# Layer 0 of a two-layer backbone: v and the output gate computed with tokens as the stationary operand, two heads at a time

## The chip, the core and the metric

The kernel runs on one core of a Trainium2 chip (trn2). The metric is the device time of one execution in microseconds (us). The kernel before took 1768.49 us, the median of three runs (1768.12 to 1774.79). The engines are named as the profile names them: PE (TensorE, matrix products; PEld is its weight load), DVE (VectorE), ACT (ScalarE), POOL (GpSimd) and SP (SyncE, which issues most of the DMAs).

## The reference, cut to what matters

512 latent tokens and 256 context tokens of width 2048 pass two layers; everything is float32. The change lies in layer 0 alone:

```
proj = xm @ w_in                       # xm: modulated tokens, 512 latent and 256 context
q, k, v, o, z_m, gates, u_p, z_p = split(proj)   # q, k, v, o, z_m: 4 heads x 256 columns each
q, k = silu(conv3(q)), silu(conv3(k))  # over three neighbouring tokens, channel by channel
h  = mlstm(q, k, v, gates)             # both directions; latent tokens also read the context's k, v
h  = h * sigmoid(o);  h = normalize(h) * g;  y_m = h * silu(z_m)
r  = multiscale_pool(u_p) - u_p        # 4 groups x 256 columns
y_p = (r @ pool_w) * pool_scale * silu(z_p)
x  = layer_norm(alpha * x + gate * (concat(y_m, y_p) @ w_out))
```

Layer 1 (a gated MLP with its own two large products) is not touched. Only the latent stream is returned, so of the context layer 0 needs k and v alone.

## The kernel before, in words

**Products on split operands.** A float32 product is made of three faster ones. `split` (L103 to L106) writes the rounded part of an operand as a `fp32r` tile (hi, on ACT, L105) and the rest as another (lo, on DVE, L106). A product is then hi·hi + hi·lo + lo·hi, three matmuls into one PSUM bank. A PSUM bank holds 128 x 512 float32; there are eight.

**Two forms.** `form_a` (L174 to L191) keeps a 128 x 128 block of weights as the stationary operand and moves tokens past it: 512 latent columns (`xh`, `xl`) and, where asked, 256 context columns (`cy`). Its result lies channels by tokens. `form_b` (L193 to L223) keeps 128 tokens as the stationary operand and moves 512 columns of weights: its result lies tokens by channels, one PSUM bank for each group of 128 tokens. Before the change `form_b` serves only the output products of both layers (L201 to L203).

**The weight stream.** The list `stream` fixes the order in which weights come from HBM, 512 KB a piece. `ahead` (L151 to L172) keeps three pieces in flight (tag `wraw`) and splits two halves of a piece ahead of the product that uses them (tag `whl`, four buffers).

**Layer 0.** While the tokens are being modulated (the first 228 us) some blocks of q, k and v are formed beside it, the list `nb1`. Then `kv_products` forms k and v of the context, and for heads 2 and 3 those of the latent tokens with them, and stores them in DRAM (`kcd`, `vcd`, `h2d`). v comes out channels by tokens and must lie tokens by channels, so `v_out` turns it by PE transposes, 128 x 128 each (L472), and splits the result. Then come the four heads. Each loads or forms q and k, forms u, o, z_m and z_p by `form_a`, and runs `attention`, `finish` and `pooling` beside these products. o is turned by PE transposes too (L724). `pooling` ends in four plain float32 products (L782) which the profile lists as two matmul records each.

**What sets the order.** `Flow` interleaves the tasks by a count of PE time: a task that yields 4.0 goes on when products worth 4 us have been emitted. A scheduler then fixes each engine's order with a simulation of its own, and gives tiles their buffers; on the chip every engine runs its list strictly in that order. `ada` is a task that streams the modulation weights of the next stages (`adat`, 512 KB for every 2.8 us of PE time at first) past a DVE multiply (L280).

**After layer 0** come its output product, layer 1's products and the final output product; their code is unchanged, but line numbers move.

## Time and profile before

| | |
|---|---|
| median of three runs | 1768.49 us |
| the profiled execution | 1771.65 us, of which span 1769.9 us |
| PE busy | 1725.7 us, 98% of the span |
| DVE busy | 1168.8 us, 66% |
| ACT busy | 686.7 us, 39% |
| chain that ended last | PE 78%, DMA 12%, DVE 7%, issue 2%, ACT 1% |
| HBM traffic | 340.93 MB read, 22.07 MB written, 205 GB/s over the span |

The profile comes from one execution, so sums made from it are set against its own 1771.65 us. Matmuls are pipelined: the duration of one record reaches into the next, so the cost of a matmul is the distance from its start to the next start. The profile's mean duration of a 128 x 512 matmul is some 390 ns, but such matmuls start every 227 ns. The span falls into the modulation stage (0 to 227.8 us), the context products of head 0 (227.8 to 256.4), the other products of `kv_products` (256.4 to 394.6), the four heads (394.6 to 898.5) and the rest.

### The profile page before, as it was taken

The page shows a single profiled execution, that of the slowest core. Times are in us where ns is not written, and L with a number is a line of the kernel's source. Part 1 is how long each engine was busy: PE and PEld are TensorE (multiplying, and loading weights), DVE is VectorE, ACT ScalarE, POOL GpSimd, SP SyncE. Part 2 cuts the span into 40 slices and gives each one's busy share as a digit, 9 for nine tenths or more (in the row PEclk, how much of TensorE's full clock was granted, in tenths as well). Part 3 has the DMA queues.
Part 4 walks back from the last instruction along what each step waited for, and adds up shares of the span by engine and source line. Part 5 has one row for each costly group of instructions (what it writes and reads, how often), then busy time and mean ns, then how long its engine had stood idle before and what let it go on. Part 6 is the DMA issues. An engine that isn't in the chain of part 4 may idle for free.

```text
span 1769.9 us, 23424 instructions
## 1 busy us (share of the span) xinstructions
PE 1725.7 (98%) x8608; PEld 1415.4 (80%) x8608; DVE 1168.8 (66%) x2074; ACT 686.7 (39%) x1209; POOL 93.9 (5%) x129
## 2 busy tenths in 40 slices
PE   8999999999999999999999999989999999999996
PEld 5677788888788888888888888878887888788884
DVE  3545598678774676875654476856776767665557
ACT  3222332124454445345342237734454354432220
POOL 0000000000000000000000000121100001000004
PEclk9999999999999999999999999999999999999998
DMA  9986289899742364663275457897757575765442
GB/s 368 358 307 236 90 310 328 295 328 363 240 149 81 118 218 148 207 216 110 84 259 152 146 187 279 225 227 198 213 158 213 147 234 128 214 158 172 134 132 106
DMA packets 133817, 364.54 MB, mean 206 GB/s; under 512 B 13262, under 2 KB 23462, under 8 KB 133190
## 3 DMA queue, kind: packets, MB, share of 16 engines
q1 hardware_dynamic: 122182, 323.20, 53.5%
q0 software_dynamic: 9216, 33.56, 10.7%
q10 hardware_dynamic: 2304, 6.29, 0.9%
q8 instruction: 67, 1.10, 0.2%
q14 instruction: 48, 0.39, 0.1%
HBM read 340.93 MB, written 22.07 MB: 205 GB/s over the span
## 4 chain that ended last, share of the span: by engine, by line
PE 78%; DMA 12%; DVE 7%; issue 2%; ACT 1%; POOL 0%; SPq 0%; POOLq 0%; DVEq 0%; ACTq 0%
DMA adw<-in_adat_dram 7%; PE ps L1211 7%; PE ps L1210 7%; PE ps L1212 7%; PE ps L190 7%; PE ps L185 7%; PE ps L186 7%; PE ps L201 6%; PE ps L203 6%; PE ps L202 6%; DMA qr<-in_wq_dram 2%; DVE adw L280 2%; PE ps L408 2%; PE ps L410 2%; PE ps L409 2%; PE ps L640 2%
## 5 line engine op out<-in xcount | busy, mean ns | idle before, releaser
L105 ACT CAST wh<-wr 128x512 fp32r<-128x512 f32 x352 | 216.4, 621 | 427.9 <-PE ps L203 164.5
L106 DVE TENSOR_TENSOR wh<-wr,wh 128x512 fp32r<-128x512 f32 x344 | 235.0, 687 | 205.0 <-ACT wh L105 199.6
L185 PE MATMUL ps<-xh,wh 128*128 128x512 f32 x704 | 278.6, 396 | 0.0
L190 PE MATMUL ps<-xh,wh 128*128 128x512 f32 x704 | 275.4, 391 | 0.3 <-DVE wh L106 0.3
L186 PE MATMUL ps<-xl,wh 128*128 128x512 f32 x704 | 275.7, 392 | 0.0
L203 PE MATMUL ps<-wh,yl 128*128 128x512 f32 x512 | 199.5, 390 | 0.0
L201 PE MATMUL ps<-wh,yh 128*128 128x512 f32 x512 | 193.6, 391 | 0.0
L202 PE MATMUL ps<-wh,yh 128*128 128x512 f32 x480 | 187.2, 390 | 0.0
L280 DVE SCALAR_TENSOR_TENSOR adw<-adw,crow 128x1024 f32<-128x1024 f32 x128 | 156.1, 1221 | 43.7 <-DMA adw<-in_adat_dram 43.3
L190 PEld LDWEIGHTS ps<-xh,wh 128*128 128x128 f32 x704 | 132.4, 188 | 29.2 <-DVE wh L106 0.7
L1211 PE MATMUL ps<-wh,ch 128*128 128x512 f32 x384 | 150.1, 393 | 0.8 <-DVE wh L106 0.7
L185 PEld LDWEIGHTS ps<-xh,wh 128*128 128x128 f32 x704 | 132.8, 189 | 22.1 <-issue 0.7
L186 PEld LDWEIGHTS ps<-xl,wh 128*128 128x128 f32 x704 | 132.9, 189 | 21.6 <-issue 0.7
L1212 PE MATMUL ps<-wh,ch 128*128 128x512 f32 x384 | 149.3, 392 | 0.0
L1210 PE MATMUL ps<-wh,ch 128*128 128x512 f32 x384 | 144.2, 397 | 3.6 <-ACT wh L105 3.6
L105 ACT CAST wh<-qr 128x1024 fp32r<-128x1024 f32 x96 | 100.9, 1057 | 117.4 <-DMA qr<-in_wq_dram 57.3
L106 DVE TENSOR_TENSOR wh<-qr,wh 128x1024 fp32r<-128x1024 f32 x96 | 116.6, 1220 | 33.1 <-ACT wh L105 13.4
L106 DVE TENSOR_TENSOR wh<-pair,wh 128x1024 fp32r<-128x1024 f32 x72 | 87.9, 1221 | 56.7 <-ACT wh L105 18.3
L105 ACT CAST wh<-pair 128x1024 fp32r<-128x1024 f32 x72 | 75.7, 1052 | 107.5 <-PE ps L1212 39.4
L1211 PE MATMUL ps<-wh,xn 128*128 128x512 f32 x288 | 113.9, 396 | 0.7 <-DVE wh L106 0.7
L1212 PE MATMUL ps<-wh,xn 128*128 128x512 f32 x288 | 113.3, 393 | 0.0
L1210 PE MATMUL ps<-wh,xn 128*128 128x512 f32 x288 | 108.0, 399 | 4.3 <-ACT wh L105 4.3
(298 smaller groups left out, 2915.4 us busy)
## 6 DMA issues: line engine op xcount, KB each, us to landing
adw<-in_adat_dram SPq DMA_DIRECT2D x128, 512.0 KB, 5.8
qr<-in_wq_dram SPq DMA_DIRECT2D x112, 512.0 KB, 4.9
wr<-in_wie_dram SPq DMA_DIRECT2D x96, 512.0 KB, 4.4
aw<-in_a_dram SPq DMA_DIRECT2D x64, 512.0 KB, 7.2
pair<-in_wq_dram POOLq DMA_DIRECT2D x56, 512.0 KB, 7.1
wr<-in_woe_dram SPq DMA_DIRECT2D x40, 512.0 KB, 4.6
wr<-in_woo_dram SPq DMA_DIRECT2D x32, 512.0 KB, 3.8
w<-in_wie_dram SPq DMA_DIRECT2D x28, 256.0 KB, 5.6
```

The source lines that it names most:

```text
L105: sc.copy(hi, src)
L106: return ve.tensor_tensor(lo, src, f32(hi), ALU.subtract)
L185: te.matmul(pt[:, :n], a, xh_, start=first, stop=False)
L186: te.matmul(pt[:, :n], a, xl_, start=False, stop=False)
L190: te.matmul(pt[:, :n], b, xh_, start=False, stop=last)
L201: te.matmul(pts[t], a, wh, start=n == 0, stop=False)
L202: te.matmul(pts[t], a, wl, start=False, stop=False)
L203: te.matmul(pts[t], b, wh, start=False, stop=n == KB - 1)
L280: ve.scalar_tensor_tensor(ts[n], ts[n], 0.5, crow[k], ALU.mult, ALU.mult, accum_out=part[:, f % 4, k:k + 1])
L1210: te.matmul(pts[t], a, wh[:, s], start=first, stop=False, **more)
L1211: te.matmul(pts[t], a, wl[:, s], start=False, stop=False, **more)
L1212: te.matmul(pts[t], b, wh[:, s], start=False, stop=end, **more)
```

## The change

- v of heads 0 and 1 is formed in one `form_b` over all six groups of 128 tokens (two of context, four latent), 512 columns at once, and v of heads 2 and 3 in a second one (`v_products`). The result is split straight from PSUM and stored in DRAM (`vd`), from which each head loads its part. `v_copy`, `v_out`, `vl_out` and the transposes of v are gone.
- o is formed by `form_b` over the four latent groups, for heads 0 and 1 while head 0 is worked on, for heads 2 and 3 in head 2. The tanh goes from PSUM straight into `og`; `o_out` and its transposes are gone.
- The pooling product is made of split operands: six `fp32r` matmuls in place of two float32 ones for each of its two banks. Three more splits for each head make the operands.
- `nb1` holds q and k of heads 1 and 2 in place of v of head 0 and k, v, q of head 1. `k_products` forms k of heads 0 and 3 only; q of head 3 alone is formed in its head.
- z_p of head 0 moves into head 1, z_p of head 2 into head 3; weights of v and o lie in DRAM as whole rows (`wv`, `wo`), the stream follows the new order.

```diff
+    Z_M, U_P, Z_P = 16, 24, 32
+    stream = a_raws(io["wie"], 8) + a_raws(io["wie"], 9) + b_raws(io["wv"], 0)
+    stream += a_raws(io["wie"], 14) + a_raws(io["wie"], 15) + b_raws(io["wv"], 1)
...
-        nb1 = [16, 17, 10, 11, 18, 19, 2, 3]
+        nb1 = [2, 3, 10, 11, 12, 13, 4, 5]
...
         def ctx_in(h):
             for j in range(2):
                 dma.dma_start(f32(kT[h][j][2]), kcd[h][:, j])
-                dma.dma_start(f32(vv[h][j][0]), vcd[h][:, j])
+                for J2 in range(3):
+                    dma.dma_start(f32(vv[h][j][J2]), vd[h, J2][:, j])
...
-            yield 1.0
-            pv = ps()
-            for j in range(4):
-                te.transpose(pv[:, j * P:(j + 1) * P], to[:, j * P:(j + 1) * P], ident)
-            ve.tensor_copy(ogt[h][:, :, fb * P:(fb + 1) * P], pv.rearrange("p (j f) -> p j f", f=P))
...
+            pws = at.tile([P, 3, 2, 256], F32R, tag="aT", name=nm("pws"))
+            split(pwt, pws[:, 0], pws[:, 1])
...
+                split(r_.rearrange("p r c -> p (r c)"), *rr[fb])
...
-                for k2 in range(2):
-                    te.matmul(pt, pwt[:, k2, fb * P:(fb + 1) * P], rr[k2].rearrange("p r c -> p (r c)"),
-                              start=k2 == 0, stop=k2 == 1)
+                for n, (k2, a, b) in enumerate((k2, a, b) for k2 in range(2) for a, b in ((0, 0), (0, 1), (1, 0))):
+                    te.matmul(pt, pws[:, a, k2, fb * P:(fb + 1) * P], rr[k2][b], start=n == 0, stop=n == 5)
...
+        def x_stat(kb, t):
+            if t < 2:
+                return cy[kb][:, 0, t * P:(t + 1) * P], cy[kb][:, 1, t * P:(t + 1) * P]
+            return xh[kb][:, (t - 2) * P:(t - 1) * P], xl[kb][:, (t - 2) * P:(t - 1) * P]
+
+        def v_products(c):
+            for pts in form_b(range(6), x_stat, range(KB)):
+                for t, pt in pts.items():
+                    vs = at.tile([P, 2, 512], F32R, tag=("og", "zs", "b0")[t % 3], name=nm("vs"))
+                    split(pt, vs[:, 0], vs[:, 1])
+                    for i in range(2):
+                        sc.dma_start(vd[2 * c + i, t // 2][:, :, t % 2, :], f32(vs[:, :, i * 256:(i + 1) * 256]))
...
+            if h in (0, 3):
+                v_products(h // 3)
...
-            for b in (4, 5, 0, 1, 2, 3) if early else (2, 3, 4, 5, 0, 1):
-                fb, out_ = b % 2, (q_out, k_out, vl_out)[b // 2]
+            for b in (0, 1, 2, 3) if early else (2, 3, 0, 1):
+                fb, out_ = b % 2, (q_out, k_out)[b // 2]
...
+                ogt[h // 2] = at.tile([P, 4, 512], F32, tag="og", name=nm("og"))
+                for pts in form_b(range(NT), lambda kb, t: x_stat(kb, t + 2), range(KB)):
+                    for t, pt in pts.items():
+                        sc.activation(ogt[h // 2][:, t, :], pt, AF.Tanh, scale=0.5)
```

Three places in the engines' orders show the moves. First PE at the end of head 0's context products. Before, `ps_2379` is the last of four banks of 256 context columns, `vs_2377` is v of head 0 on its way to the transposes, and `ps_2485` and `ps_2486` are the first banks of head 2:

```order
L190 MATMUL ps_2379<-cy_1189,wh_2382 128x256
L472 MATMUL ps_2432<-ident,vs_2377 128x128 [waits DMAHW0_49,Activation_49]
L185 MATMUL ps_2379<-cy_1319,wh_2400 128x256
L190 MATMUL ps_2379<-cy_1319,wh_2400 128x256 [waits DVE_49]
...
L190 MATMUL ps_2379<-cy_1629,wh_2400 128x256
L472 MATMUL ps_2477<-ident,vs_2455 128x128 [waits Activation_49]
L185 MATMUL ps_2485<-cy_167,wh_2417 128x256
L185 MATMUL ps_2486<-xh_165,wh_2417 128x512
```

Now `ps_2210` is the second and last bank of head 0's k, and `ps_2291` to `ps_2296` are the six banks of v:

```order
L191 MATMUL ps_2210<-cy_1627,wh_2231 128x256
L203 MATMUL ps_2291<-wh_2248,cy_165 128x512 [waits DVE_49]
L203 MATMUL ps_2292<-wh_2248,cy_165 128x512
L203 MATMUL ps_2293<-wh_2248,xh_163 128x512
L204 MATMUL ps_2293<-wh_2248,xl_164 128x512
L203 MATMUL ps_2296<-wh_2248,xh_163 128x512
L202 MATMUL ps_2291<-wh_2266,cy_225 128x512 [waits Activation_49]
```

The transposes between the products are gone, and one half of a weight piece (`wh_2248`) now serves eighteen matmuls of 512 columns in place of twelve of 256.

Second, ACT right behind the first group of v, in the kernel after alone (`vs` are the split results, `wh` halves of weights to come, DMAHW the counters of earlier DMAs):

```order
L105 CAST vs_2766<-ps_2293 128x512 [waits PE_49]
L798 DMA vd<-vs_2756 256x1x256 [waits DMAHW1_49,DVE_49]
L798 DMA vd<-vs_2761 256x1x256 [waits DMAHW3_49,DVE_49]
L798 DMA vd<-vs_2766 256x1x256 [waits DMAHW6_49]
L105 CAST wh_2861<-wr_2635 128x512 [waits PE_49]
L105 CAST wh_2893<-wr_2688 128x512 [waits PE_49]
L105 CAST vs_2771<-ps_2294 128x512 [waits DMAHW2_49,DMAHW1_49]
L798 DMA vd<-vs_2771 256x1x256 [waits DMAHW3_49,DVE_49]
L105 CAST wh_2923<-wr_2688 128x512 [waits PE_49]
```

The fourth of the six results, `vs_2771`, reuses the first one's buffer, so its cast waits until that one's store has landed, and the hi half `wh_2923` stands behind it. Before, the stores of v (`vcd`) stood in ACT's list with no cast waiting for them.

Third, PE in the attention of head 0, where row block 0's six transposes end and row block 1's scores begin. Before (`ps_4020` is the one bank that o's product holds):

```order
L190 MATMUL ps_4020<-xh_417,wh_3982 128x512
L707 MATMUL ps_4039<-ident,w_3914 128x128 [waits DVE_49,PE_49]
L707 MATMUL ps_4040<-ident,w_3914 128x128 [waits PE_49]
L648 MATMUL ps_4051<-qkv_3667,qkv_3663 128x512 [waits PE_49]
L649 MATMUL ps_4052<-qkv_3669,qkv_3663 128x256 [waits PE_49]
```

Now (`ps_3809` is the last of the four banks that o's product holds at the same time):

```order
L204 MATMUL ps_3809<-wh_3861,xl_511 128x512
L689 MATMUL ps_3915<-ident,w_3793 128x128 [waits DVE_49,PE_49]
L689 MATMUL ps_3916<-ident,w_3793 128x128 [waits PE_49]
L630 MATMUL ps_3927<-qkv_3570,qkv_3566 128x512
L631 MATMUL ps_3928<-qkv_3572,qkv_3566 128x256
```

The sequence is the same; o's four banks, the transposes' two and the scores' two make eight, which is all that PSUM has.

## Rows read from the trace of the kernel before

**Rows 1.** The page's first part: busy time, share of the span and instructions of each engine.

```profile
PE 1725.7 (98%) x8608; PEld 1415.4 (80%) x8608; DVE 1168.8 (66%) x2074; ACT 686.7 (39%) x1209; POOL 93.9 (5%) x129
```

**Rows 2.** The table by stretches of time: length, busy time and instructions of each engine, then the granted clock of PE (1.00 is full), the DMA engines' busy share and GB/s.

```profile
227.80:256.40 28.60, 24.61 (x199) 23.80 (x198) 27.38 (x56) 13.56 (x29) 0.00 (x0) 1.00 0.92 332
256.40:394.60 138.20, 137.31 (x784) 118.35 (x783) 103.60 (x232) 34.60 (x77) 0.00 (x0) 1.00 0.90 315
394.60:898.50 503.90, 499.65 (x2438) 415.33 (x2437) 346.92 (x775) 227.02 (x493) 7.76 (x34) 1.00 0.54 178
```

**Rows 3.** PE's groups by line and shape: count, busy us, mean ns of one, idle time before them; here the transposes of v (L472), of o (L724), and of the pooling product (L782).

```profile
L472 PE MATMUL ps<-ident,v 128*128 128x128 f32 x24 | 3.1, 272 | 0.0
L472 PE MATMUL ps<-ident,vs 128*128 128x128 f32 x12 | 2.4, 282 | 1.6 <-ACT vs L464 1.6
L472 PE MATMUL ps<-ident,h 128*128 128x128 f32 x8 | 1.0, 272 | 0.0
L472 PE MATMUL ps<-ident,accs 128*128 128x128 f32 x4 | 0.6, 272 | 0.0
L724 PE MATMUL ps<-ident,tt 128*128 128x128 f32 x32 | 4.8, 272 | 0.0
L782 PE MATMUL ps<-pr,pwt 128*128 128x512 f32 x32 | 14.4, 592 | 0.0
```

**Rows 4.** PE's timeline (start, duration, instruction) around eight transposes of v and around head 1's pooling product.

```profile
629.34 0.39 PE L190 MATMUL ps<-xh,wh 128*128 128x512 f32 x1
629.58 1.03 PE L472 MATMUL ps<-ident,v 128*128 128x128 f32 x8
630.37 0.48 PE L185 MATMUL ps<-xh,wh 128*128 128x512 f32 x1
630.68 0.40 PE L186 MATMUL ps<-xl,wh 128*128 128x512 f32 x1
...
634.06 3.60 PE L782 MATMUL ps<-pr,pwt 128*128 128x512 f32 x8
637.09 0.79 PE L185 MATMUL ps<-xh,wh 128*128 128x512 f32 x1
637.73 0.40 PE L186 MATMUL ps<-xl,wh 128*128 128x512 f32 x1
```

**Rows 5.** PE's timeline, first and last of 25 start-to-start distances in `form_a` with 512 columns (first pair) and of 18 in `form_b` (second pair).

```profile
402.21 0.39 PE L186 MATMUL ps<-xl,wh 128*128 128x512 f32 x1
407.90 0.39 PE L190 MATMUL ps<-xh,wh 128*128 128x512 f32 x1
...
944.75 0.39 PE L201 MATMUL ps<-wh,yh 128*128 128x512 f32 x1
948.83 0.39 PE L201 MATMUL ps<-wh,yh 128*128 128x512 f32 x1
```

**Rows 6.** PE's timeline in the context products: first and last of 58 distances with 256 columns alone; then first and last of nine equal periods of context and latent tokens together (three matmuls of 256 columns and three of 512 each).

```profile
238.52 0.28 PE L186 MATMUL ps<-cy,wh 128*128 128x256 f32 x1
245.47 0.28 PE L186 MATMUL ps<-cy,wh 128*128 128x256 f32 x1
...
257.66 0.28 PE L185 MATMUL ps<-cy,wh 128*128 128x256 f32 x1
267.13 0.28 PE L185 MATMUL ps<-cy,wh 128*128 128x256 f32 x1
```

**Rows 7.** PE's timeline, the records with idle time before them (in brackets, with what ended it).

```profile
238.30 0.39 PE L185 MATMUL ps<-cy,wh 128*128 128x256 f32 x1 [1.51 <-ACT wh L105]
246.40 0.39 PE L185 MATMUL ps<-cy,wh 128*128 128x256 f32 x1 [0.65 <-ACT wh L105]
248.57 0.39 PE L190 MATMUL ps<-cy,wh 128*128 128x256 f32 x1 [0.48 <-DVE wh L106]
255.89 0.44 PE L472 MATMUL ps<-ident,vs 128*128 128x128 f32 x2 [1.34 <-ACT vs L464]
400.82 0.44 PE L472 MATMUL ps<-ident,vs 128*128 128x128 f32 x2 [0.27 <-ACT vs L464]
484.23 2.93 PE L640 MATMUL ps<-qkv,aT 128*128 128x256 f32 x16 [2.01 <-DVE aT L712]
```

**Rows 8.** The costliest groups on ACT and DVE: the two halves of a weight split.

```profile
L105 ACT CAST wh<-wr 128x512 fp32r<-128x512 f32 x352 | 216.4, 621 | 427.9 <-PE ps L203 164.5
L106 DVE TENSOR_TENSOR wh<-wr,wh 128x512 fp32r<-128x512 f32 x344 | 235.0, 687 | 205.0 <-ACT wh L105 199.6
```

**Rows 9.** DMA issues by line: queue, count, KB each, median us from issue to landing; and one 40 us stretch of the table by stretches.

```profile
wr<-in_wie_dram SPq DMA_DIRECT2D x96, 512.0 KB, 4.4
wr<-in_woe_dram SPq DMA_DIRECT2D x40, 512.0 KB, 4.6
vcd<-vo ACTq DMA_DIRECT2D x4, 512.0 KB, 10.9
h2d<-hl ACTq DMA_DIRECT2D x8, 256.0 KB, 6.0
...
400.00:440.00 40.00, 39.43 (x189) 32.49 (x188) 35.39 (x72) 19.48 (x43) 0.00 (x0) 1.00 0.97 366
```

**Rows 10.** The groups of attention's bank evacuation, ACT and DVE, in the heads' stretch (394.6 to 898.5).

```profile
L711 ACT ACTIVATE aT<-ps 128x512 fp32r<-128x512 f32 (+1 forms) x32 | 14.0, 486 | 4.3 <-PE ps L707 4.3
L712 DVE SCALAR_TENSOR_TENSOR aT<-ps,aT 128x512 fp32r<-128x512 f32 (+1 forms) x32 | 16.6, 550 | 0.6 <-ACT aT L711 0.6
```

141 lines of the change are left out of this document (48 added, 93 removed).

## The prediction

> **What bounds the kernel now.** I read the page's busy times first, then the table by stretches, then PE's timeline with its idle times, and last the DMA issues. PE is busy 1725.7 of 1769.9 us [rows 1], and no other engine comes near it. The table by stretches shows the same where the change lies: PE idles 28.60 - 24.61 = 4.0 us in head 0's context products, 138.20 - 137.31 = 0.9 us in the rest of them and 503.90 - 499.65 = 4.3 us in the four heads [rows 2]. The granted clock reads 1.00 in all three, the 2.4 GHz level. So in 670.7 us PE waits 9.1 us: here a matmul taken away is time taken away, unless its removal opens a new wait. Two things could open one. The DMA engines are busy 0.92 and 0.90 of the first two stretches, and DVE 27.38 of 28.60 us in the first [rows 2].
>
> **Equal columns, other shapes.** The change moves no column away: v of 8 blocks was formed with tokens moving, and is now formed with weights moving. In units of 48 matmuls for each block of 128 channels, before the change the main loop had: 4 blocks of 256 context columns alone, 8 of context and latent together, 4 of q (heads 2 and 3) and 8 of o with 512 columns. Alone, 256 columns start every 6.95/58 = 0.1198 us; a period of both takes 9.47/9 = 1.052 us, 16 of them a block [rows 6]; 512 columns in `form_a` start every 5.69/25 = 0.2276 us and in `form_b` every 4.08/18 = 0.2267 us [rows 5]. That is 4 x 48 x 0.1198 + 8 x 16 x 1.052 + 12 x 48 x 0.2276 = 23.0 + 134.7 + 131.1 = 288.8 us. After it there are 2 blocks of k of head 0 alone (11.5), 2 of k of head 3 with both (33.7), q of head 3 (96 x 0.2276 = 21.8), v with 2 x 6 x 48 = 576 matmuls (130.6) and o with 384 (87.1): 284.7 us. Term 1: **-4.1 us**. The modulation stage forms eight blocks before and after, four of them with context, so it stays.
>
> What each form costs in the trace is a price per column: 0.1198 us for 256 columns, twice that is 0.2396 against 0.2267 [rows 5, 6]. The Trainium skill ("TensorE: Matmul & The Clock Gate", section "Back-to-back issue gap") gives 262 cycles for 256 columns and 518 for 512 of an isolated matmul at full clock, so joining two of 256 would save 6 cycles. By it the 192 joined pairs would give back some 0.5 us, an estimate from that page, and term 1 would nearly vanish. The rows differ from it and decide.
>
> **Transposes.** The records are 24 + 12 + 8 + 4 = 48 of v and 32 of o [rows 3], all gone. Eight of them between two products push the next-but-one start from two steps of 0.2276 us to 630.68 - 629.34 = 1.34 us [rows 4]: 0.885 us for eight, 0.1106 for one, the change of kind before and after included. They stand in PE's list between products that wait for nothing else, so nothing hides them. Term 2: 80 x 0.1106 = **-8.8 us**.
>
> **Pooling.** A head's float32 products hold PE from 634.06 to 637.73 less one ordinary step, 3.44 us [rows 4]; twelve `fp32r` matmuls at 0.2267 us take 2.72 us. Term 3, four heads: **-2.9 us**. The operands cost three more splits a head, at 0.62 us on ACT and 0.69 on DVE [rows 8], together 7.4 and 8.2 us. Against them go six casts of v on ACT and eight copies of o on DVE. Both engines have room: DVE is busy 346.92 of 503.90 us in the heads [rows 2], and a head's splits lie beside the 20 us of z_p, u or q that follow its attention. If that cover were gone PE would wait one chain of 1.3 us for each head, 5 us in all.
>
> **Idle time.** Four of the idle times end by v itself: 1.34 and 0.27 us for a cast before a transpose, 0.65 and 0.48 us for weight halves [rows 7]. The last two come because twelve matmuls of 256 columns use up a half in 1.44 us while DVE is full; a half of v's weights now serves eighteen matmuls, 4.08 us. Term 4: **-2.7 us**. The 1.51 us at 238.30 I keep, since the first eight halves go to k of head 0 as eight halves went to it before. The 2.01 us at 484.23 belong to attention of head 0, I keep them too.
>
> **What it adds.** Each v group ends with six full banks, split into three buffers and stored by twelve DMAs of 256 KB in pieces of 1 KB on ACT's queue. The fourth cast waits for the first store to land, and weight halves are queued behind it on ACT; PE waits for these. No row shows a store in such pieces. The nearest rows are 6.0 us (256 KB, `h2d`) and 10.9 us (512 KB, `vcd`) to landing [rows 9]. Behind the first group five halves are cast ahead of the waiting one, at 16 x 1.052 / 4 = 4.2 us of products each, 21 us: more than either. Behind the second group six halves of u's weights go first, at 12 x 0.2276 = 2.7 us each, 16.4 us; three casts, one DVE split and 10.9 us make some 14 us, so the cover has 2 us left. Lower bound 0. Upper bound: a landing of twice the longest row, 21.8 us, leaves PE waiting some 4 us behind the first group and 8 us behind the second, 12 us. I take **+2 us**, near the lower end, because the nearest row of the same size is 6.0 us. Loads of v now come by six DMAs a head in place of two and of the two that carried raw v; all of them are issued 20 to 40 us of products ahead of the value products that read them, and rows in long pieces and in pieces of 2 KB land alike (4.4 and 4.6 us [rows 9]), so the new layout of the weights costs nothing. z_p's move swaps equal products. The other bank user, o's product holding four banks for 192 x 0.2267 = 43.5 us while attention runs, I cost at nothing (rival 3).
>
> **The sum.** -4.1 - 8.8 - 2.9 - 2.7 + 2 = -16.5 us. From the profiled execution's own 1771.65 us that gives 1755.2; the shown median is 3.2 us lower, and from 1768.49 the forecast is **1752 us**, with a range of its own of 1747 to 1758.
>
> **Rivals.**
> 1. *The stores hold the weights up.* For it: the DMA engines are at 0.97 and 366 GB/s in the 40 us where head 0 begins [rows 9], just where the second burst of 3 MB now falls. Against it: PE still idles little there, and the cover above. Price: the upper bound of 12 us in place of 2, so 1762. The Trainium skill ("DMA: Bandwidth & Descriptors", section "Issuing engines are not separate DMA queues") says that transfers issued by ACT and by SP share the same 16 engines and interleave, which speaks for this rival: a store on ACT's queue takes its share from the weights. No run here yet shows how much.
> 2. *DMA, not PE, paces the context products.* Then what is saved there does not come back: term 1 (4.1 us) and the 16 context transposes (1.8 us). For it 0.90 of DMA time [rows 2], against it that PE idles 0.9 us in 138. Time: 1752 + 6 = 1758.
> 3. *Slower: PSUM runs short in heads 0 and 2.* o holds four of eight banks, so a row block's transposes and the next scores fill the rest, and every row block would wait for an evacuation, a cast of 0.49 us on ACT and 0.55 us on DVE for each of two banks, 2.1 us [rows 10], once before the scores and once before the values: 8 x 2 x 2.1 = 34 us, 1786. It decides from 16.5 / 8 = 2.1 us per row block, one full evacuation. Against it: in the new order two weight halves (5.4 us) stand between the transposes and the values, and the scores are placed directly behind the transposes with no wait for ACT or DVE.
> 4. *More is gained.* If the two waits that I kept vanish (1.51 and 2.01 us [rows 7]) and the new ones cost nothing: -16.5 - 2 - 3.5 = -22, 1746.
>
> **How the numbers follow.** Forecast 0.64, rival 1 0.12, rival 2 0.09, rival 3 0.05, rival 4 0.10. A measurement of this kernel tells 0.5%, some 9 us, from no change: faster means below 1759.6. The forecast, rivals 2 and 4 and a quarter of rival 1 lie there, 0.86, rounded to 0.85; the rest of rival 1 is 0.10 of no change; rival 3 is 0.05 of slower. The range from 1743 to 1762 holds all but rival 3, the upper half of rival 1 and the edges.
>
> **What the profile after would show.** Right: no `v` or `tt` transposes; the v products starting every 0.227 us; the heads' stretch some 471 us long (503.9 less 21.8 of q, which goes early, 66 transposes of 0.11 and 2.9 of pooling) with PE idling 4 to 6 us in it; the time from 227.8 us to the first output product 654 us in place of 670.7. Wrong: PE idling before matmuls that wait for ACT's `wh` in the 20 us behind either group of v (rival 1); DVE waiting for `adw` with PE idling behind it (rival 2); PE waiting for an evacuation before L630 or L622 in heads 0 and 2 (rival 3). A price per matmul above 0.23 us in v would break term 1.

## The result and the profile after

The changed kernel takes 1749.0 us (median of 4 runs, 1746.5 to 1750.2) against 1769.1 us for the kernel before (4 runs), a ratio of 0.9878 with a 95% interval of 0.9854 to 0.9903. It is faster, by some 20 us; the forecast was 1752. The profiled execution took 1746.46 us with a span of 1744.7 us. Medians and ratios here and below are those of fast executions; one execution each of e8 (3179.34 us), e10 (8357.07) and e11 (1897.01) was slow and is left out.

The page's first part answers to [rows 1]: 256 matmuls fewer, and PE busy 17.7 us less.

```profile
PE 1708.0 (98%) x8352; PEld 1398.6 (80%) x8352; DVE 1165.6 (67%) x2058; ACT 683.7 (39%) x1189; POOL 94.6 (5%) x129
```

The table by stretches (columns as in [rows 2]) of the changed kernel: k of head 0, then the rest of the context products with both groups of v, then the heads, and in the last row all three.

```profile
228.60:239.20 10.60, 10.42 (x87) 10.22 (x85) 10.01 (x19) 4.09 (x8) 0.00 (x0) 1.00 0.91 319
239.20:411.00 171.80, 171.76 (x804) 142.74 (x805) 137.28 (x293) 47.49 (x95) 0.00 (x0) 1.00 0.96 333
411.00:874.70 463.70, 461.35 (x2271) 388.07 (x2270) 325.38 (x730) 219.82 (x475) 7.97 (x34) 1.00 0.55 182
228.60:874.90 646.30, 643.73 (x3161) 541.21 (x3160) 472.88 (x1041) 271.60 (x577) 7.97 (x34) 1.00 0.66 224
```

I call the stretch of the last row the main phase: from the first context product to the first output product. It lasts 646.3 us; before, it lasted 670.7, of which PE was busy 661.6 (the sum of [rows 2], 24.61 + 137.31 + 499.65). So the main phase gave 24.4 us, and all the rest of the span 0.8. Of the 24.4, PE's busy time gave 17.9 and its idle time 6.5 (9.1 to 2.6).

PE's timeline of the main phase holds only three records with more than 0.15 us of idle time before them; they answer to [rows 7]:

```profile
239.24 0.73 PE L202 MATMUL ps<-wh,cy 128*128 128x512 f32 x2 [0.22 <-ACT wh L105]
416.35 0.50 PE L186 MATMUL ps<-xh,wh 128*128 128x512 f32 x1 [1.16 <-ACT wh L105]
429.87 0.50 PE L191 MATMUL ps<-xh,wh 128*128 128x512 f32 x1 [1.13 <-DVE wh L106]
```

The first stands where 1.51 us stood before. The waits inside v and the 2.01 us of head 0's attention are gone. The other two are new: both lie behind the second group of v, and both are for weight halves.

Four more waits of the kernel before are gone, which [rows 7] leaves out: 0.89 us at 369.94 and 0.31 at 413.81, both for weight halves, and two in head 0's attention. The six in [rows 7] and these four make up the 9.1 us. The two in attention:

```profile
456.33 0.87 PE L707 MATMUL ps<-ident,w 128*128 128x128 f32 x6 [0.90 <-DVE w L701]
464.27 2.22 PE L640 MATMUL ps<-qkv,aT 128*128 128x256 f32 x16 [0.77 <-DVE aT L712]
```

The first and last of the second group's 288 products, and the first and the last product of one head's pooling with the product behind it (they answer to [rows 5] and [rows 4]):

```profile
341.42 0.40 PE L202 MATMUL ps<-wh,cy 128*128 128x512 f32 x1
406.64 0.39 PE L204 MATMUL ps<-wh,xl 128*128 128x512 f32 x1
...
637.04 0.47 PE L760 MATMUL ps<-prh,pws 128*128 128x512 f32 x1
639.68 0.39 PE L760 MATMUL ps<-prh,pws 128*128 128x512 f32 x1
639.91 0.40 PE L186 MATMUL ps<-xh,wh 128*128 128x512 f32 x1
```

v's products start every 65.22 / 287 = 0.2272 us. A head's pooling holds PE for 2.87 us in place of 3.44. The new stores answer to [rows 9]: issues by line, here those between 405 and 432 us.

```profile
vd<-vs ACTq DMA_DIRECT2D x12, 256.0 KB, 6.5
```

One more view of the kernel before belongs here. The table by stretches of 2 us, right behind the wait of 2.01 us in head 0, shows TensorE's granted clock (third number from the end) at 0.50, the 1.2 GHz level:

```profile
483.80:485.80 2.00, 1.57 (x11) 1.57 (x12) 2.00 (x6) 0.00 (x0) 0.00 (x0) 0.88 0.34 130
485.80:487.80 2.00, 2.00 (x9) 1.82 (x9) 2.00 (x8) 0.00 (x0) 0.00 (x0) 0.50 0.00 0
487.80:489.80 2.00, 2.00 (x8) 1.62 (x7) 1.71 (x9) 1.36 (x4) 0.00 (x0) 0.77 0.43 131
```

That is 2 x (0.12 + 0.50 + 0.23) = 1.7 us of work lost behind a wait of 2.0, and it is counted as busy time. The stretch of the heads in [rows 2] shows 1.00, since 1.7 in 504 us rounds away. No stretch of the changed kernel's main phase shows less than 1.00. Right ahead of it, though, the clock of the changed kernel fell as well, behind 24 small products for the gates and with no wait of PE before it. PE's timeline, and the table by stretches:

```profile
221.35 2.82 PE L522 MATMUL ps<-ga,sel 32*56 32x128 f32 x24
...
224.00:226.00 2.00, 2.00 (x7) 1.51 (x6) 2.00 (x4) 0.00 (x0) 0.00 (x0) 0.56 0.84 180
226.00:228.00 2.00, 2.00 (x7) 1.57 (x6) 1.47 (x5) 0.00 (x0) 0.00 (x0) 0.59 1.01 366
```

That is 2 x (0.44 + 0.41) = 1.7 us of work lost outside the main phase; the kernel before shows 1.00 there. It bears on the wait before the first v product, further down.

### The profile page after: what moved, and what is told of

Its sections match the earlier page's. It is cut to its first block, busy times and chain, and to the rows that moved or that the text cites. A ratio compares the mean times of both kernels' runs of the same rounds, so it can differ in the third digit from the quotient of the medians.

```text
span 1744.7 us, 22883 instructions
## 1 busy us (share of the span) xinstructions
PE 1708.0 (98%) x8352; PEld 1398.6 (80%) x8352; DVE 1165.6 (67%) x2058; ACT 683.7 (39%) x1189; POOL 94.6 (5%) x129
## 4 chain that ended last, share of the span: by engine, by line
PE 76%; DMA 13%; DVE 7%; issue 2%; ACT 1%; ACTq 0%; POOL 0%; SPq 0%; POOLq 0%; DVEq 0%
PE ps L202 8%; PE ps L204 8%; PE ps L203 8%; PE ps L1179 7%; PE ps L1180 6%; PE ps L1178 6%; DMA adw<-in_adat_dram 5%; PE ps L191 5%; PE ps L186 5%; PE ps L187 5%; DMA qr<-in_wq_dram 3%; DVE adw L279 2%; PE ps L407 2%; PE ps L409 2%; PE ps L408 2%; PE ps L622 2%
## 5 line engine op out<-in xcount | busy, mean ns | idle before, releaser
L105 ACT CAST wh<-wr 128x512 fp32r<-128x512 f32 x344 | 211.4, 621 | 461.7 <-PE ps L204 251.4
L106 DVE TENSOR_TENSOR wh<-wr,wh 128x512 fp32r<-128x512 f32 x336 | 229.6, 687 | 193.5 <-ACT wh L105 191.8
L279 DVE SCALAR_TENSOR_TENSOR adw<-adw,crow 128x1024 f32<-128x1024 f32 x128 | 155.5, 1219 | 34.3 <-DMA adw<-in_adat_dram 34.2
L186 PE MATMUL ps<-xh,wh 128*128 128x512 f32 x448 | 175.7, 392 | 1.2 <-ACT wh L105 1.2
L191 PE MATMUL ps<-xh,wh 128*128 128x512 f32 x448 | 174.9, 390 | 1.2 <-DVE wh L106 1.1
L187 PE MATMUL ps<-xl,wh 128*128 128x512 f32 x448 | 174.8, 390 | 0.0
L106 DVE TENSOR_TENSOR wh<-qr,wh 128x1024 fp32r<-128x1024 f32 x96 | 116.5, 1219 | 33.3 <-ACT wh L105 13.0
L106 DVE TENSOR_TENSOR wh<-pair,wh 128x1024 fp32r<-128x1024 f32 x72 | 87.8, 1220 | 55.3 <-PE ps L1179 19.8
L204 PEld LDWEIGHTS ps<-wh,yl 128*128 128x128 f32 x512 | 96.1, 188 | 20.0
L202 PEld LDWEIGHTS ps<-wh,yh 128*128 128x128 f32 x512 | 96.0, 188 | 19.7
L203 PEld LDWEIGHTS ps<-wh,yh 128*128 128x128 f32 x480 | 90.1, 188 | 18.4
```

The costliest lines, as they stand in the source:

```text
L105: sc.copy(hi, src)
L106: return ve.tensor_tensor(lo, src, f32(hi), ALU.subtract)
L186: te.matmul(pt[:, :n], a, xh_, start=first, stop=False)
L187: te.matmul(pt[:, :n], a, xl_, start=False, stop=False)
L191: te.matmul(pt[:, :n], b, xh_, start=False, stop=last)
L202: te.matmul(pts[t], a, wh, start=n == 0, stop=False)
```

## The experiments

All ran on the chip beside the kernel before. Main phase, PE's busy and idle time in it are from the profile of one execution; effects of 2 us are read there, since the intervals of the ratios are some 0.2% (4 us) to either side. Four runs with the same products (changed, e2, e8, e12) have PE busy 642.4 to 644.0 us once the half clock in e8 (1.7 us) is taken off, so busy times are good to some 1.5 us. The rest of the span, which the experiments hardly touch, differs from 1097.4 to 1103.8 us between the profiled executions, so a total need not follow its main phase.

| run | main phase | PE busy | PE idle | median us | ratio to before, 95% |
|---|---|---|---|---|---|
| before | 670.7 | 661.6 | 9.1 | 1769.1 | 1 |
| changed | 646.3 | 643.7 | 2.6 | 1749.0 | 0.9878 [0.9854, 0.9903] |
| e1_pool_plain | 651.2 | 646.5 | 4.7 | 1751.9 | 0.9894 [0.9871, 0.9916] |
| e2_prl_free | 648.1 | 644.0 | 4.1 | 1749.8 | 0.9882 [0.9858, 0.9905] |
| e3_before_es_late | 663.8 | 658.9 | 4.9 | 1768.8 | 0.9985 [0.9970, 0.9999] |
| e4_o_turned | 649.5 | 647.0 | 2.5 | 1753.0 | 0.9892 [0.9876, 0.9909] |
| e5_v_halves | 651.6 | 649.9 | 1.6 | 1754.4 | 0.9907 [0.9887, 0.9928] |
| e6_store_twice | 659.3 | 647.5 | 11.8 | 1762.8 | 0.9953 [0.9937, 0.9970] |
| e7_v_alone | 657.0 | 652.2 | 4.7 | 1757.9 | 0.9922 [0.9904, 0.9941] |
| e8_one_store | 647.4 | 644.0 | 3.4 | 1749.4 | 0.9876 [0.9859, 0.9894] |
| e9_five_bufs | 652.4 | 644.6 | 7.8 | 1750.4 | 0.9892 [0.9866, 0.9918] |
| e10_one_store_adw_pool | 659.6 | 648.0 | 11.6 | 1760.1 | 0.9946 [0.9929, 0.9962] |
| e11_store_pool | 654.7 | 648.0 | 6.8 | 1758.1 | 0.9944 [0.9924, 0.9964] |
| e12_one_store_d2 | 642.5 | 642.5 | 0.0 | 1748.6 | 0.9892 [0.9870, 0.9914] |

### The wait of 2.01 us in head 0

The theory is that PE waited for an evacuation that stood behind another step in DVE's order: a multiplication on the next head's row tiles `es`, whose load was still on its way. In the kernel before, DVE's timeline shows that step and the evacuations behind it:

```profile
483.28 0.29 DVE L670 TENSOR_TENSOR em<-es,kc 128x128 f32<-128x128 f32 x1 [4.35 <-DMA es<-ed]
483.49 1.02 DVE L712 SCALAR_TENSOR_TENSOR aT<-ps,aT 128x512 fp32r<-128x512 f32 x2
```

**es late in the kernel before.** A tiny tile holds the buffer of `es` until pooling is through:

```diff
+            dm = at.tile([P, 8], F32, tag="r0", name=nm("dm"))
+            ve.tensor_copy(dm[0:1, 0:8], rr[1][0:1, 0, 0:8])
```

> The kernel before the change with one edit: a copy of 8 numbers that reads the last pooling operand and holds the buffer of the next head's row tiles (es) until pooling is through. Nothing is computed otherwise. Theory A: DVE's step on the next head's es no longer stands before head 0's last evacuations; the wait of 2.01 us of PE in head 0 goes, the main phase shrinks from 670.7 to 668.7 us, and the ratio to the kernel before is 0.9989. Rival B: the place of that step is not what PE waited for; then the 2.01 us stay and the ratio is 1.000. A third outcome: the es tiles now come late for the next head and DVE or PE waits for them there, by up to the 4.4 us that DVE waited for them before.

DVE's and PE's timelines now: the evacuations come at once, and the products behind them carry no idle time.

```profile
476.24 1.01 DVE L712 SCALAR_TENSOR_TENSOR aT<-ps,aT 128x512 fp32r<-128x512 f32 x2
479.46 2.08 PE L640 MATMUL ps<-qkv,aT 128*128 128x256 f32 x16
```

The 16 products take 2.08 us, not 2.93 as in [rows 7], because the clock stays at full level. The wait and the 1.7 us behind it are gone. The rest of the 6.9 us in the main phase lies at places that the edit doesn't touch, among them the 1.51 us at 238.30. The two shorter waits of the same attention did not go: in place of 0.90 and 0.77 us they are 1.46 and 1.12 us here. By medians the run gained 0.15%. DVE waits for `es` in the next head now, 6.0 us, and PE does not.

**es early in the changed kernel.** The lo part of the first pooling operand (`prl`) gets its own buffer.

```diff
-                           at.tile([P, NL], F32R, tag="r0", name=nm("prl"))))
+                           at.tile([P, NL], F32R, tag="prl", name=nm("prl"))))
```

> The changed kernel with one edit: the second part of the pooling operand gets a buffer of its own, so the row tiles (es) of the next head can load before pooling is through. Nothing is computed otherwise. Theory A: one DVE step on the next head's es stands again before head 0's last evacuations and waits for the load; PE idles about 2.0 us there, main phase 648.1 in place of 646.1, PE busy unchanged at 643.5. Rival B (the wait of 2.01 us went with DVE's lighter work): main phase 646.1, no wait of PE for DVE's aT over 0.5 us. Total 1751 by A, 1749 by B, which the total alone can't tell apart, so the listed waits decide.

DVE's timeline in it, and then PE's last score and first value products of the same row block:

```profile
485.35 0.29 DVE L652 TENSOR_TENSOR em<-es,kc 128x128 f32<-128x128 f32 x1 [3.09 <-DMA es<-ed]
486.16 1.02 DVE L694 SCALAR_TENSOR_TENSOR aT<-ps,aT 128x512 fp32r<-128x512 f32 x2
```

```profile
486.00 0.28 PE L631 MATMUL ps<-qkv,qkv 128*128 128x256 f32 x1
491.60 2.31 PE L622 MATMUL ps<-qkv,aT 128*128 128x256 f32 x18
```

The step is back in front of the evacuations and waits 3.09 us. But PE has 24 products of o to do from 486.11 to 491.60, and `aT` is ready at 487.18.

So theory A, as it was put for the changed kernel, fell, and was mended to A2: late `es` or enough products of o between scores and values, either is enough. The first half is shown by e3, and it is what the changed kernel has: SP issues the load of `es` at 495.60 there, behind this attention, so the step can't stand in front.

The second half is not shown. With the 13 products of o that the kernel before had between scores and values (3.0 us), PE would have come to the values at 489.1 in e2, still behind `aT`. What differs is the load. In the kernel before it is issued at 476.83, 2.0 us before the scores end (478.84), and DVE's step starts 4.4 us after their end; in e2 it is issued at 479.88, 6.2 us before their end (486.11), and the step starts 0.8 us before it. What moved the issue was not tested.

### What the parts are worth

**Pooling back.** Edit of the changed kernel:

```diff
-                te.matmul(pt, pws[:, a, k2, fb * P:(fb + 1) * P], rr[k2][b], start=n == 0, stop=n == 5)
+                te.matmul(pt, pwt[:, k2, fb * P:(fb + 1) * P], rr[k2]..., start=k2 == 0, stop=k2 == 1)
```

> The changed kernel with the pooling product as plain float32 products, as before the change; the new order, v and the output gate stay. Term 3 (pooling worth 2.9 us over four heads) expects PE's busy time in the main phase (from the first context product to the first output product, 646.1 us after the change, PE busy 643.5, idle 2.5) to rise by 2.9 us. Theory A on the vanished wait of 2.01 us in head 0's attention: the new operand buffer of the pooling product keeps the next head's row tiles (es) from loading early, so DVE's first step on them no longer stands in front of head 0's last evacuations; without that buffer the step stands there again and PE idles about 2 us before the product that reads aT, 4.4 to 4.9 us longer in all, main phase 651. Rival B: the wait went because DVE has less to do or came to another place; then no such wait, main phase 649. In the total, A 1754 and B 1752 beside 1749 for the changed kernel.

PE's busy time rose by 2.75 us, against 2.9: term 3 stands, to the 1.5 us given above. No wait for `aT` came back, though `es` is early here: A fell, as in the run before. The rest of the 4.9 us is idle time, nearly all of it at the three places that the changed kernel has too.

**The output gate back.** In the changed kernel, o as before: `form_a`, 32 transposes, copies.

```diff
-                for pts in form_b(range(NT), lambda kb, t: x_stat(kb, t + 2), range(KB)):
...
+                for i in range(4):
+                    pt = ps()
+                    form_a([(pt, lat)])
+                    t_o.append(fl.spawn(o_out(pt, h + i // 2, i % 2)))
```

> The changed kernel with the output gate o formed as before (weights stationary, 32 PE transposes and the copies behind them, in its old place beside attention); the new v and the new pooling product stay. By terms 1 and 2, 32 x 0.1106 = 3.5 us of transposes and 384 x 0.0009 = 0.3 us for the other form: PE's busy time in the main phase 647.6 in place of 643.7. On the vanished wait of head 0 the theory is now A2, from the two runs before (late es tiles alone removed it from the kernel before; early es tiles alone did not bring it back to the changed kernel): either the late es tiles or the two weight halves of o (5.4 us) between scores and values are enough to remove it. Then no wait of 2 us for aT here, main phase 650.2. Rival: the o of before alone brings it back, with the half clock behind it, main phase 654. Total 1753 or 1757.

Busy time rose by 3.3 us against 3.8: (3.3 - 0.3) / 32 = 0.094 us a transpose in place of 0.1106, which the spread of busy times can't tell apart. No wait of 2 us for `aT` came back; `es` is late here, as in the changed kernel.

**v and the order alone.** Both of these edits together.

> The changed kernel with o as before and the pooling product as before: v and the order of the heads' work alone. The parts add up if PE's busy time in the main phase is 643.7 + 2.75 (pooling, as run) + 3.9 (o, expected) = 650.3. Here es tiles load early and o has its old shape, so by A2 the wait for aT in head 0 comes back, in part: 20 products of o (4.6 us) stand between scores and values in place of 13 (3.0 us) in the kernel before, so 0.4 to 2.0 us of idle time, and if it reaches some 2 us, the half clock behind it with 2 us more. Main phase 653 to 657. If neither es nor o is the cause, no wait and 653. Total 1755 to 1759, against 1769 before: v and the order are then worth more than half of the gain.

The main phase is 657.0 us as the upper end said, but the half clock in it stands elsewhere: behind a wait of 1.82 us for a weight half at 419.53, after the second v group.

```profile
419.65:421.65 2.00, 2.00 (x6) 1.31 (x7) 2.00 (x3) 1.34 (x3) 0.00 (x0) 0.73 1.11 391
421.65:423.65 2.00, 2.00 (x7) 1.52 (x6) 1.50 (x4) 0.12 (x1) 0.00 (x0) 0.50 1.04 360
423.65:425.65 2.00, 2.00 (x10) 1.62 (x9) 0.00 (x0) 0.00 (x0) 0.00 (x0) 0.92 1.03 416
```

Less the 1.7 us that it lost there (2 x (0.27 + 0.50 + 0.08)), PE is busy 650.5 us: the parts add up (650.3 expected; 649.8 with o at its measured 3.3). Against the kernel before without its own half clock, 661.6 - 1.7 = 659.9, v and the order are worth 9.4 us of busy time. The forecast's terms give 3.8 + 48 x 0.1106 = 9.1.

The wait for `aT` did not come back, where A2 expected 0.4 to 2.0 us of it. DVE does wait 2.94 us for `es`, and its evacuations end at 492.6; but the value products stand at 495.39, 20 products of o behind the scores in place of 13:

```profile
490.19 0.29 DVE L653 TENSOR_TENSOR em<-es,kc 128x128 f32<-128x128 f32 x1 [2.94 <-DMA es<-ed]
491.60 1.01 DVE L695 SCALAR_TENSOR_TENSOR aT<-ps,aT 128x512 fp32r<-128x512 f32 x2
```

It is not the distance that decided. With 13 products behind the end of the scores (490.81) PE would have come at 493.8, still after 492.6. As in e2 the load of `es` was early against PE's work: DVE's step starts 0.6 us before the scores end.

**v in columns of 256.** Each matmul of v cut in two over one stationary tile.

```diff
+            if cut:
+                for x_, w_ in ((a, wh), (a, wl), (b, wh)):
+                    for s_ in (slice(0, 256), slice(256, 512)):
+                        te.matmul(pts[t][:, s_], x_, w_[:, s_], ...)
```

> The changed kernel with every matmul of v cut into two of 256 columns over the same stationary tile: 1152 in place of 576, and nothing else. By the rows of the trace before (256 columns start every 0.1198 us, 512 every 0.2267) v costs 576 x (0.2396 - 0.2267) = 7.4 us more, main phase 653.5, total 1756. If a second matmul on the same stationary tile needs no new load that limits it, or if DMA or the weight halves and not PE pace these products, less than 2 us more, total 1749 to 1751. The Trainium skill ("TensorE: Matmul & The Clock Gate", section "Back-to-back issue gap") gives 262 cycles for 256 columns and 518 for 512, by which 576 x 6 cycles at 2.4 GHz would be 1.4 us, an estimate from that page.

From its first product to its last, the first group takes 70.55 us in place of 67.13, the second 68.97 in place of 65.22: 7.2 us more, against 7.4. The rows' price per column holds, and term 1 with it. Each half came with a weight load of its own (8928 matmuls and 8928 loads in the page, 576 more of each), so what a second half costs without one is not shown. By the figures for an isolated matmul in the Trainium skill ("TensorE: Matmul & The Clock Gate", section "Back-to-back issue gap") it would have been 1.4 us, an estimate from that page; the run disagrees, with 7.2. The main phase grew by 5.3 us only: the 2.3 us of waits behind the second group went, probably because the slower products gave the weights time, while the wait before the first product was 1.52 us in place of 0.22.

### The waits behind the second v group

**Every store twice.** The second copy goes into a DRAM tile that nothing reads.

> The changed kernel with every store of v issued twice, the second copy into a DRAM tile that nothing reads. Behind the second group of v PE waits 1.16 and 1.13 us for weight halves in the changed kernel. Theory C: the issue of the stores on ACT's queue holds the weight casts that are queued behind them (six of them took 4.84 us of it at 410.79); twelve take twice that, PE's idle time behind the second group grows by about 4.8 us, to 7, and by 0 to 4 us behind the first. Theory D (rival 1): the bytes do it; 3 MB more for each group at the 366 GB/s of that stretch is 8.6 us of DMA time, weights land late and PE idles behind both groups, some 8 us each. Cover theory: the halves cast ahead hide it, under 2 us in all. Total 1754 by C, 1762 or more by D, 1750 by cover.

PE waited behind both groups:

```profile
325.51 0.58 PE L186 MATMUL ps<-cy,wh 128*128 128x256 f32 x1 [5.12 <-ACT wh L105]
426.65 0.50 PE L186 MATMUL ps<-xh,wh 128*128 128x512 f32 x1 [3.24 <-ACT wh L105]
445.63 1.20 PE L202 MATMUL ps<-wh,xh 128*128 128x512 f32 x4 [1.35 <-ACT wh L105]
```

9.7 us in all, with the half clock behind the longer two; the time came to 1762.8, as D said, though PE waited less than D's 8 us behind each group (5.1 and 4.6 us) and behind the second also less than C's 7. But twice the stores are twice the bytes and twice the issues, so this alone doesn't settle which. Two more runs and the last one of all do.

**One store for each bank**, the same bytes in the same pieces, half the issues:

```diff
-                    for i in range(2):
-                        sc.dma_start(vd[2 * c + i, t // 2][:, :, t % 2, :], f32(vs[:, :, i * 256:(i + 1) * 256]))
+                    sc.dma_start(vd[2 * c:2 * c + 2, t // 2].rearrange("i p j b f -> p j b i f")[:, :, t % 2],
+                                 f32(vs).rearrange("p j (i f) -> p j i f", i=2))
```

> The changed kernel with one store of 512 KB for each bank of v in place of two of 256 KB: six issues a group in place of twelve, the same bytes in the same pieces. Theory C (issue time on ACT's queue): ACT is free for the weight casts 2.4 us earlier behind the second group, the first of the two waits there (1.16 us) goes, PE's idle time behind it falls from 2.3 to about 1.1 us, main phase 645. Theory D (the landing of the bytes, or DVE's late splits, set it): no change, 2.3 us of idle time, main phase 646.3. The total can't tell these apart (1748 or 1749); the listed waits decide.

**Five buffers** for the second group, so that fewer casts wait for a landing:

```diff
-                    vs = at.tile([P, 2, 512], F32R, tag=("og", "zs", "b0")[t % 3], name=nm("vs"))
+                    vs = at.tile([P, 2, 512], F32R, tag=(("og", "zs", "b0") * 2, ("og", "zs", "b0", "b2", "b1", "og"))[c][t], name=nm("vs"))
```

> The changed kernel with five buffers for the split banks of the second v group in place of three, so that the fourth and fifth cast don't wait for a store to land; twelve issues as in the changed kernel. Theory C (issue time on ACT's queue, about 0.8 us an issue, holds the weight casts): six issues still stand before the weight casts, PE's idle time behind the second group stays near 2 us (1.2 to 3). Theory D (the wait for the landing holds them): the casts go through and the idle time behind the second group falls to under 0.5 us. The total tells nothing (1747 to 1749).

ACT's timeline behind the second group (ACTq is its queue of DMA issues), in the changed kernel:

```profile
410.79 4.84 ACTq L798 DMA_DIRECT2D vd<-vs  x6
415.68 1.66 ACT L105 CAST wh<-wr 128x512 fp32r<-128x512 f32 x3 [10.06 <-DVE adw L279]
418.17 0.59 ACT L105 CAST vs<-ps 128x512 fp32r<-128x512 f32 x1 [0.83 <-DMA vd<-vs]
420.73 2.87 ACTq L798 DMA_DIRECT2D vd<-vs  x2
423.64 0.59 ACT L105 CAST vs<-ps 128x512 fp32r<-128x512 f32 x1 [4.88 <-DMA vd<-vs]
```

DVE's timeline of the same place (L106 on `vs` is its half of v's split):

```profile
410.07 1.88 DVE L106 TENSOR_TENSOR vs<-ps,vs 128x512 fp32r<-128x512 f32 x3
```

ACT's timeline with one store a bank:

```profile
410.68 2.59 ACTq L797 DMA_DIRECT2D vd<-vs  x3
413.31 1.14 ACT L105 CAST wh<-wr 128x512 fp32r<-128x512 f32 x2 [4.07 <-DVE adw L279]
```

and with five buffers, with PE's record of that place behind it:

```profile
412.67 7.57 ACTq L798 DMA_DIRECT2D vd<-vs  x8
420.76 1.14 ACT L105 CAST wh<-wr 128x512 fp32r<-128x512 f32 x2
```

```profile
421.44 0.80 PE L186 MATMUL ps<-xh,wh 128*128 128x512 f32 x1 [6.15 <-ACT wh L105]
```

An issue takes 4.84 / 6 = 0.81 us of ACT's queue, 2.59 / 3 = 0.86 and 7.57 / 8 = 0.95. With three issues in front of them the weight casts come at 413.31, and both of PE's waits are gone, the second too. The missing waits alone prove little, since PE came 3.6 us later in this run (the group's last product stands at 410.26, in the changed kernel at 406.64). The last run below (e12) is the better test. It has one store a bank too, ends the group at 406.62 and has no wait; of the 2.4 us by which its casts come earlier than in the changed kernel 2.0 are the issues, and 0.4 the earlier start of DVE's half (409.67). PE's and ACT's timelines:

```profile
406.62 0.39 PE L204 MATMUL ps<-wh,xl 128*128 128x512 f32 x1
...
410.39 2.79 ACTq L797 DMA_DIRECT2D vd<-vs  x3
413.23 1.66 ACT L105 CAST wh<-wr 128x512 fp32r<-128x512 f32 x3 [7.63 <-DVE adw L279]
```

With five buffers eight issues stand in front, the casts come at 420.76 and PE waits 6.15 us, where C expected 1.2 to 3 us and D less than 0.5. The casts are 5.1 us later than in the changed kernel: 2.7 of it are the two more issues, 1.9 the later start of the issues behind DVE's half of the split, and 0.5 a cast of v ahead of them. So the casts follow the issues that stand ahead of them, not the bytes (unchanged) and not the buffers (more of them made it worse): theory C. DVE's share comes on top: the issues can't start before its half of the split, which stands behind multiplications that wait for `adw`. In time the one store gained nothing that can be told: the wait before the first v product was 3.37 us in its profile, with 1.7 us of half clock behind it, and that place is next.

### The wait before the first v product, and a version to beat both

Where the kernel before waited 1.51 us and the changed one 0.22, the other runs with the same first stage waited 0.60, 1.46, 1.82, 1.52, 1.51, 1.59, 3.37 and 1.62 us (e1, e2, e4 to e9). So the 1.3 us that the changed kernel's profile won here are a matter of the execution, not of the change.

The granted clock tells these executions apart. In five of the fourteen profiled ones (the changed kernel, e3, e10, e11 and e12) it fell to 0.50 for some 3.5 us between 224 and 229 us, behind the 24 small products shown above; in the other nine it reads 1.00 there. The five waited 0.22 us or not at all at this place, the nine 0.60 us and more. PE simply came later in the five: their main phases begin at 228.3 to 229.1 us, those of the nine at 227.0 to 228.0. What the wait takes in the nine, the half clock (1.7 us) has taken just before in the five. This is a match over fourteen executions; no run forced the clock either way.

**adw on POOL's queue**, on top of one store a bank:

```diff
-                dma.dma_start(t, io["adat"][f_, :, k_ * 1024:(k_ + 1) * 1024])
+                gp.dma_start(t, io["adat"][f_, :, k_ * 1024:(k_ + 1) * 1024])
```

> The kernel with one store for each bank (run before) and one more edit: the row loads of the second modulation (adw) are issued on POOL's queue in place of SP's. It tests what the idle time before the first v product (238.30 in the kernel before, 239 to 241 in the others, 0.2 to 3.4 us) is. Theory E: SP's issue of an adw load waits for DVE to free its buffer (5.05 us of SP's queue at 235.12 in the run with one store, 2.57 at 235.23 in the changed kernel), and the loads of v's weights are queued behind it; on another queue they go out in time, the wait falls under 0.3 us, main phase 644 to 645 in place of 647.4, total 1746 and so faster than both kernels by some us. Theory F: the bytes themselves are late, since the DMA engines are busy 0.9 there; then the wait stays between 0.2 and 3.4 us. Theory G: POOL issues slower or its loads land later, DVE waits for adw and delays the weight halves; main phase 648 or more, total above 1751.

The wait at 239 went, and worse came: theory G. DVE's waits for `adw` between 228 and 470 us add up to 51.9 us (34.2 in the changed kernel), its half of the splits came late, and PE waited 5.88 us behind the second group. DVE's waits (us in total, times, longest) and PE's timeline:

```profile
DVE adw L279 <- DMA adw<-in_adat_dram: 51.9, 39, 3.4
```

```profile
425.40 0.80 PE L191 MATMUL ps<-xh,wh 128*128 128x512 f32 x1 [5.88 <-DVE wh L106]
```

**v's stores on POOL's queue** (one a bank, `gp.dma_start` in place of `sc.dma_start`):

> The kernel with one store for each bank of v and one more edit: these stores are issued on POOL's queue, so that no store stands among ACT's casts. Theory C: nothing but the landing of an earlier store is left in front of the weight casts behind the second v group, so PE doesn't wait there (idle 0 to 0.3 us, as with one store on ACT's queue), and ACT's pause of 10 us before them (it waited in its queue for DVE's half of the split) shrinks too. Main phase 644 plus the wait before the first v product, which this edit doesn't touch (0.2 to 3.4 us so far): 644 to 648, total 1747 to 1750. Rival: stores from POOL's queue land later, the fourth cast waits longer for its buffer and holds the weight casts behind it; idle time behind the second group 2 us or more, total 1751 or more.

The rival: ACT's weight casts went out on time at first, but the fifth cast of the second group waited 8.52 us for a landing with weight casts behind it, and PE waited 2.19 us there, with the half clock after it. ACT's timeline:

```profile
421.76 0.59 ACT L105 CAST vs<-ps 128x512 fp32r<-128x512 f32 x1 [2.15 <-DMA vd<-vs]
430.87 0.58 ACT L105 CAST vs<-ps 128x512 fp32r<-128x512 f32 x1 [8.52 <-DMA vd<-vs]
```

A longer wait of PE, 3.88 us and again with the half clock after it, is of another kind. It stands among the first products of the second group and is for a PSUM bank that DVE had still to read for the gates (`xb`); v's six banks leave two of the eight:

```profile
348.44 0.79 PE L202 MATMUL ps<-wh,xh 128*128 128x512 f32 x1 [3.88 <-DVE xb L591]
```

The same wait is 0.23 us in e2, 0.73 in e7 and 1.35 in e10, and the changed kernel has none. Whether the new queue lengthened it here was not tested, so not all that this run lost is shown to be the stores'.

This run had no wait before the first v product, although nothing there was changed; so neither e10 nor the next run shows what that wait is.

**adw two ahead**, with one store a bank: `ADA_D = 2` in place of 3.

> The kernel with one store for each bank of v (on ACT's queue) and one more edit: the rows of the second modulation (adw) are fetched two ahead in place of three, in the same three buffers, so that SP's issue of such a load finds its buffer free for a whole step longer. Theory E (SP's queue waits for DVE to free the buffer, and v's weights are queued behind): the wait before the first v product falls under 0.3 us and no half clock follows it. Theory G: DVE now waits longer for adw (34.2 us in all in the changed kernel) and delays the weight halves and its half of v's split; PE waits at other places by 2 us or more. By E alone main phase 644 and total 1746, by G 648 or more and 1751 or more.

PE idles nowhere in the main phase:

```profile
229.10:871.60 642.50, 642.50 (x3161) 541.54 (x3160) 472.46 (x1040) 272.56 (x578) 7.93 (x34) 1.00 0.66 225
```

The main phase is 3.8 us shorter than the changed kernel's, the shortest of all, but the rest of the span is 5.4 us longer in this execution (1103.8 against 1098.4). The medians don't show a gain (1748.6 against 1749.0, the intervals of the ratios lie over each other), so as a version it is level with the changed kernel. The sign of theory E, no wait before the first v product, came true, but SP's issue of the adw loads before v's weights took 2.57 us as in the changed kernel, and the half clock stood just ahead here as in the other runs without the wait. So theory E has no support.

## Why the prediction was right, and where it fell short

The direction, the place and the mechanism were right; the gain was 4 to 8 us larger than the 16.5 forecast (20 by medians, 24.4 in the main phase of the profile). By the steps:

- *Terms 1 to 3* summed to -15.8 us of busy time, and 17.9 went. 1.7 of the difference is the half clock behind the wait of 2.01 us, which was in the kernel before and which the prediction didn't see: it read the clock over whole stretches, where it shows 1.00 [rows 2]. Against 659.9 us the fall is 16.2. Singly: pooling 2.75 (2.9 forecast), o 3.3 (3.8), v and order 9.4 (9.1).
- *Term 4*, -2.7: these four waits ended by v itself and are gone. Two more for weight halves, 0.89 and 0.31 us at 369.94 and 413.81, which I had not listed, went too.
- *The two waits kept* is the step that failed. I kept 2.01 us "in attention of head 0" without asking what DVE did there; its timeline shows the load of `es`, and the diff shows a new tile in that buffer (`prl` in `r0`), behind which the load now goes out. With two smaller ones in the same attention (0.90 and 0.77 us at 456.33 and 464.27) 3.7 us of waits went, and with the clock 5.4. What ended the two smaller ones is not shown: late `es` alone left them (e3). The 1.51 us shrank to 0.22 in one profile that had lost 1.7 us to the half clock just before; with the clock at 1.00 there the wait stayed.
- *What it adds*, +2: 2.29 us were found, right behind the second group, where the cover was put at 2 us. The size was right by luck: I priced the landing of the stores, and it is their issue on ACT's queue, with DVE's late half ahead of it. By my account five buffers would have helped; they made it worse.
- *Rival 1* had the right place and queue. That its upper bound of 12 us is about what doubled stores cost (main phase +13.0) is a coincidence, since it was worked out for the stores as they are. The Trainium skill ("DMA: Bandwidth & Descriptors", section "Issuing engines are not separate DMA queues") says that another issuing engine saves only the sequencer's time to initiate, usually small beside the transfer. Here that time decided: 0.8 us an issue, six in front of a cast.
- *Rival 2* fell: DMA is busy 0.96 in the context stretch, yet PE idles 0.04 us in its 171.8. Its sign, DVE waiting for `adw` with PE idling behind it, shows only in a part of the 2.3 us behind the second group. *Rival 3* fell: PE waits for no evacuation in heads 0 and 2. *Rival 4* (1746) lies as far from 1749.0 as the forecast does and nearer by the main phase (22 us against 24.4), with half of its reason: the wait in head 0 went, the new waits did cost.

The marks: 0.227 us a product of v, as said; the heads' stretch 463.7 us in place of 471 and idle 2.4 in place of 4 to 6; 646.3 us from the first context product in place of 654.

## What to carry to other kernels

Before a wait is put down as "kept", follow it on the engine that it names to the instruction in front of the one waited for: an early step of the next piece of work in an in-order engine can hold a late step of this one, and a buffer that is shared or freed moves it. Count the DMA issues that stand in an engine's own order ahead of work that others wait for, before counting bytes. Read the granted clock in stretches of 2 us around each wait of PE, since a wait can be paid a second time there, and also just ahead of the phase that is compared: there it moved a wait out of the phase and its cost with it.

## What the runs showed of the hardware

- TensorE's clock fell to the 1.2 GHz level around waits of 2.01 (before), 1.82 (e7), 2.19 and 3.88 (e11), 3.24 and 5.12 (e6), 3.37 (e8), 5.88 (e10) and 6.15 us (e9), between matmuls that were otherwise dense, and cost 1.7 us of work behind the shortest two. It did not fall behind 1.94 us (e1) and another 1.82 (e4).
- It also fell, with no wait of PE, behind 24 small products that took 2.82 us: in five of fourteen executions, for some 3.5 us and 1.7 us of work each.
- A store of 256 KB takes about as long to issue on ACT's queue (0.81 us) as one of 512 KB (0.86) in the stretch behind the second v group, in rows of six and of three. Single ones behind them took 0.52 (changed) and 0.59 us (e8). Why an issue is longer in a row is not shown.
- Two products of 256 columns over one stationary tile take 0.24 us, as long as over two; the tile was loaded again for the second.
